# Two bits per step in the sample's threshold search, and a new set of stream priorities

## The chip, the core and the metric

The kernel runs on one core of a Trainium2 chip. Time is the device time of one execution in microseconds (us); a run's time is compared with the median of several runs. An engine's clock, where it is named, is the share of its full rate that the profile shows as granted to TensorE (PE).

## The reference

A decoder of two layers takes one step for two groups of rows: a prompt of 512 rows, and a sample of 8 requests with 4 new rows each (32 rows) that have 2048 earlier keys in a paged cache. In each layer a mixer A (gated MLP) and a mixer B (sparse attention) run side by side. Mixer B is where the change lies: a light indexer scores all keys of a row, the best are kept, and attention runs over these alone.

```
def indexer_scores(qi, wi, ki):
    s = jnp.einsum('bthd,bld->bthl', qi, ki).astype(jnp.float32) * (IDX_DIM ** -0.5)
    w = wi.astype(jnp.float32) * (IDX_HEADS ** -0.5)
    return jnp.einsum('bthl,bth->btl', jax.nn.relu(s), w)
...
    I = indexer_scores(qi, wi, ki_all)        # sample: 2052 keys per row
    ...
    _, idx = lax.top_k(I, TOPK_SAMPLE)        # the 256 best (prompt: the 128 best of up to 512)
    ...
    return attend_selected(q, k_sel, v_sel, valid)
```

After the mixers come the output projection w_o, a layer norm (LN1), a squared-ReLU MLP (f1, f2) with a gate, and a second layer norm.

## The kernel before

The 544 rows are held as columns in two halves of 272. Matrices are split into a high and a low part, and three products (`mm<-hi,Ah`, `hi,Al`, `lo,Ah` and the like) make one exact product on PE; VectorE (DVE) makes the low parts (L738), ScalarE (ACT) the high ones (L732). Each layer has, in order of time: the input projection; a stretch in which the indexer scores come out and are searched; a stretch of attention "units" (softmax heads, L1607 to L1621) with the sample's own attention (`s_attn`, `s_attn_f`) and the first half of w_o (L1918); the second half of w_o (L1928), which needs the sample's attention; LN1; the MLP (some 395 us); LN2.

The prompt's top-k takes 16 rounds of MAX8 (L1248) and MATCH_REPLACE8 (L1250) on DVE for each of three blocks of 512, 384 and 256 keys, and ends in masks (L1253). The softmax of a unit (L1607 first, then L1611 on ACT, L1613 and L1617) needs such a mask, but for the first block, which has no search.

The sample's choice works in another way, in `s_scores`. All scores of a row stand in `y.I` (L1306), 513 columns on each partition with a row's keys spread over several partitions. Their 256th largest value is found bit by bit: one ACT pass gives the signs of (threshold minus score) with a sum along the row (L1321); one PE matmul with a matrix `gallf` of ones and zeros adds the sums of the partitions of a row and gives each of them the total; two DVE instructions (L1334, L1336) compare the total with a limit and set the threshold's next bit. One round for the sign and 31 for the bits are 32 rounds per layer, one behind the other. Then 0/1 masks, ties and the mask `y.maskb` follow (L1339 to L1393, 22 DVE instructions and six matmuls). PE spreads this mask over the heads in matmuls `at<-maskb,sel` and the sample's attention goes on (L1855, L1880, up to `Al` at L1830).

The order of all instructions on all engines is fixed when the kernel is built. A planner (`Sched`) holds one generator per piece of work (a stream); each yields the engine and the cost in ns of its next piece, and the planner takes, in its own reckoning of time, the streams by a priority from the table `PR` (L59). So one changed number in `PR` may move instructions of all streams on all engines. Inside `count` the cost of a Sign pass is 707 ns with a margin `MARGIN` of 500 ns behind it before the matmul may be put in PE's list.

Of the kernel before, what the change touches and what calls it, by code (L numbers as in the profile page):

```python
# [55 lines left out]
GL = 1200.0  # L56
WP = 0.928
WO = 10.5
PR = {'q_sample': 13.5, 'free_raw': 8.0, 'gmix': 7.5, 'evac_c1': 14.0, 's_scores': 17.0, 's_block': 17.5, 'mix_b': 4.5, 'load_r': 6.5, 'kidx': 7.5, 's_attn': 5.0, 'evac_au': -2.5, 'head': 1.5, 's_kt': 6.0, 'loads': 7.5, 'evac_q': -4.0, 'sgu_load': 13.5, 's_relu': 1.0, 'mix_a': 14.5, 'setup1': 8.5, 's_attn_f': 10.5, 'gmlp': 4.5, 'unit': 9.0, 'load_pe': 13.0, 'evac_oa': -0.5, 'backbone': -5.5, 'evac_c0': -3.5, 'setup2': -2.0, 'splits': -2.5, 's_qk': 3.5, 'gnorm': 3.0, 'store': 3.0, 'setup': 13.0, 'wout22': 11.5, 'wadd': 12.0, 'mtee': 4.0, 'fin': 0.5, 'wsum': 7.0, 'wcopy': 0.5, 'evac_p': 10.0, 'ln1': 2.0, 'moving': 11.5, 'vload': 2.5, 'split_x': -1.0, 'evac_f2': 0.0, 'warm': 7.5, 'wsplit': 6.0, 'mv': 5.0, 'evac_o': 9.5, 'wout': 11.5, 'ln2': 10.5, 'evac_g': 0.0}  # L59
TBS = (3, 1, 2, 0)  # L60
BIAS = 65.107
GBIAS = 422.464
# [29 lines left out]
class Sched:  # L92
# [166 lines left out]
def cQ(cols, k=1):  # L259
    return [("Q", 480.0 * k), ("D", cols * 512 / 360.0)]  # L260
# [153 lines left out]
def build(tc, I, O, cols):  # L414
    nc = tc.nc
    V, A, G, PE, SP = nc.vector, nc.scalar, nc.gpsimd, nc.tensor, nc.sync
# [13 lines left out]
    def const(name, shape, dt=F32):  # L430
        return sb.tile(list(shape), dt, tag=name, name=name)
# [18 lines left out]
    gallf = const("gallf", [128, 128])  # L450
# [89 lines left out]
    def setup2():  # L540
        st = yield Al("w", [128, 2 * NT])
        yield cQ(768)
        SP.dma_start(st[:, :768], I["cbf"][:, :768])
        S.cur.ready += 900.0
        yield [("G", 3000.0)]
        G.tensor_copy(gall, st[:, 0:128])
        G.tensor_copy(gallf, st[:, 0:128])
# [282 lines left out]
    def mm(out, l, r, start, stop):  # L830
        PE.matmul(out, l, r, start=start, stop=stop, skip_group_check=True)  # L831
# [322 lines left out]
    def evac_c0(y, bi, ps):  # L1154
# [9 lines left out]
        if bi == 0:  # L1164
# [101 lines left out]
    def s_scores(y):  # L1266
# [40 lines left out]
        S.free(pi)  # L1307
        Iv = y.I[:, :513]
        cnt = sm("cnt", [128, 1], F16)
        cf = sm("cf", [128, 1])  # L1310
        c = sm("c", [128, 1], I32)
        d = sm("d", [128, 1], I32)
        c2 = sm("c2", [128, 1])
        c3 = sm("c3", [128, 1])
        ps = yield Al("at", [128, 512])
        dp = ps[:, 8:9].bitcast(I32)
        lim = NQ - 2 * STOP + 0.5

# [33 lines left out]
        thr = c3  # L1352
# [812 lines left out]
    def backbone():  # L2165
        for y in LY:
# [300 lines left out]
```

## Time and profile before

| What | us |
|---|---|
| median of 3 runs (lowest, highest) | 1471.88 (1468.57, 1473.65) |
| profiled execution | 1471.24 |
| its span, first to last instruction | 1469.5 |
| PE busy | 1427.5 (97%) |
| DVE busy | 1083.2 (74%) |
| ACT busy | 805.4 (55%) |
| granted PE clock, mean | 0.991 |

The shares of busy time are means over stages that differ. The search of the sample's threshold runs at 80 to 178 us in layer 0 and at 807 to 912 us in layer 1; the unit stages follow up to 271 and 996 us. A stage is read in the rows of the view by stretches: busy time of every engine in it, with the number of instructions in brackets, and the clock granted to PE.

### The profile page before, as it was taken

The page shows a single profiled execution, that of the slowest core. Times are in us where ns is not written, and L with a number is a line of the kernel's source. Part 1 is how long each engine was busy: PE and PEld are TensorE (multiplying, and loading weights), DVE is VectorE, ACT ScalarE, POOL GpSimd, SP SyncE. Part 2 cuts the span into 40 slices and gives each one's busy share as a digit, 9 for nine tenths or more (in the row PEclk, how much of TensorE's full clock was granted, in tenths as well). Part 3 has the DMA queues.
Part 4 walks back from the last instruction along what each step waited for, and adds up shares of the span by engine and source line. Part 5 has one row for each costly group of instructions (what it writes and reads, how often), then busy time and mean ns, then how long its engine had stood idle before and what let it go on. Part 6 is the DMA issues. An engine that isn't in the chain of part 4 may idle for free.

```text
span 1469.5 us, 31243 instructions
## 1 busy us (share of the span) xinstructions
PE 1427.5 (97%) x12284; PEld 1363.9 (93%) x12284; DVE 1083.2 (74%) x2812; ACT 805.4 (55%) x1895; POOL 143.8 (10%) x201
## 2 busy tenths in 40 slices
PE   9999989999999999999999988999999999999997
PEld 8798877999999999999987987889999999999996
DVE  5699995797956748567676999768979476494765
ACT  6668664473733626335466777755647255271533
POOL 2113512010000000000102045020000000000000
PEclk9999989999999999999999999999999999999999
DMA  7636424122231322313344265150223323132211
GB/s 241 220 102 203 168 87 160 47 71 87 92 124 58 130 72 87 128 60 118 113 133 163 96 214 178 58 189 30 79 88 108 101 72 130 59 115 87 87 58 62
DMA packets 55475, 164.48 MB, mean 112 GB/s; under 512 B 7648, under 2 KB 15008, under 8 KB 55328
## 3 DMA queue, kind: packets, MB, share of 16 engines
q1 hardware_dynamic: 44960, 124.73, 25.4%
q0 software_dynamic: 10368, 37.75, 7.9%
q8 instruction: 96, 1.57, 0.5%
q14 instruction: 51, 0.42, 0.1%
HBM read 156.09 MB, written 6.37 MB: 111 GB/s over the span
## 4 chain that ended last, share of the span: by engine, by line
PE 79%; DVE 15%; ACT 3%; issue 1%; DMA 1%; another core or an unknown queue 0%; SPq 0%; DVEq 0%; ACTq 0%
PE at L831 40%; PE mm L831 36%; DVE u L1250 3%; DVE m L1248 3%; DVE lo L738 1%; PE at L1621 1%; DVE u L1607 1%; DVE t L968 1%; PE at L1880 1%; DVE c L1336 1%; DVE u L1577 0%; DVE t L966 0%; PE at L1713 0%; DMA Bh<-in_x 0%; DVE w L868 0%
## 5 line engine op out<-in xcount | busy, mean ns | idle before, releaser
L732 ACT CAST hi<-raw 128x1024 fp32r<-128x1024 f32 (+5 forms) x137 | 139.0, 1019 | 178.3 <-PE mm L831 90.6
L738 DVE TENSOR_TENSOR lo<-raw,hi 128x1024 fp32r<-128x1024 f32 (+5 forms) x136 | 161.9, 1190 | 36.3 <-ACT hi L732 35.7
L831 PE MATMUL mm<-Bh,hi 128*128 128x272 f32 x584 | 172.0, 294 | 2.4 <-DVE t L1029 1.3
L831 PE MATMUL mm<-Ah,hi 128*128 128x272 f32 x584 | 170.7, 292 | 0.1
L831 PE MATMUL mm<-Bl,hi 128*128 128x272 f32 x584 | 169.0, 289 | 0.0
L831 PE MATMUL mm<-Bh,lo 128*128 128x272 f32 x584 | 168.6, 289 | 0.0
L831 PE MATMUL mm<-Al,hi 128*128 128x272 f32 x584 | 168.6, 289 | 0.0
L831 PE MATMUL mm<-Ah,lo 128*128 128x272 f32 x584 | 168.1, 288 | 0.0
L831 PE MATMUL at<-w,hi 128*128 128x272 f32 x704 | 158.9, 289 | 0.0
L691 ACT CAST hi<-u 128x512 fp32r<-128x512 f32 x128 | 75.4, 619 | 97.2 <-PE mm L831 40.9
L831 PE MATMUL at<-w,lo 128*128 128x272 f32 x416 | 119.8, 288 | 0.0
L831 PEld LDWEIGHTS at<-w,hi 128*128 128x128 f32 x704 | 119.4, 188 | 0.0
L2092 DVE TENSOR_TENSOR u<-u,mm 128x272 f32<-128x272 f32 x96 | 41.8, 436 | 103.2 <-PE mm L831 102.9
L831 PEld LDWEIGHTS mm<-Bh,hi 128*128 128x128 f32 x584 | 110.5, 189 | 4.1 <-ACT wi L1160 1.7
L831 PEld LDWEIGHTS mm<-Ah,hi 128*128 128x128 f32 x584 | 109.9, 188 | 1.3 <-issue 0.8
L831 PEld LDWEIGHTS mm<-Bh,lo 128*128 128x128 f32 x584 | 110.6, 189 | 0.1
L691 ACT CAST hi<-raw 128x1024 fp32r<-128x1024 f32 x64 | 53.2, 831 | 104.2 <-PE at L831 35.5
L831 PEld LDWEIGHTS mm<-Ah,lo 128*128 128x128 f32 x584 | 110.1, 189 | 0.2
L831 PEld LDWEIGHTS mm<-Bl,hi 128*128 128x128 f32 x584 | 110.2, 189 | 0.0
L831 PEld LDWEIGHTS mm<-Al,hi 128*128 128x128 f32 x584 | 109.8, 188 | 0.0
L831 PE MATMUL at<-Bl,hi 128*128 128x272 f32 x376 | 108.7, 289 | 0.0
L831 PE MATMUL at<-Al,hi 128*128 128x272 f32 x376 | 108.7, 289 | 0.0
(394 smaller groups left out, 4313.7 us busy)
## 6 DMA issues: line engine op xcount, KB each, us to landing
raw<-in_w_f SPq DMA_DIRECT2D x128, 512.0 KB
raw<-in_w_q SPq DMA_DIRECT2D x16, 512.0 KB
raw<-in_w_o SPq DMA_DIRECT2D x16, 512.0 KB
raw<-in_w_g SPq DMA_DIRECT2D x16, 512.0 KB
raw<-in_w_au SPq DMA_DIRECT2D x8, 512.0 KB
raw<-in_w_av SPq DMA_DIRECT2D x8, 512.0 KB
u<-in_x SPq DMA_DIRECT2D x8, 272.0 KB
hD<-t SPq DMA_DIRECT2D x16, 136.0 KB
```

Source lines behind the costliest of these rows:

```text
L691: A.copy(hi[:, :n], x)
L732: A.copy(c.hi[:, a:b], c.raw[:, a:b])
L738: E.tensor_tensor(c.lo[:, a:b], c.raw[:, a:b], c.hi[:, a:b].bitcast(F32), op=ALU.subtract)
L831: PE.matmul(out, l, r, start=start, stop=stop, skip_group_check=True)
L968: V.tensor_tensor(t[:, :n], t[:, :n], pb[:, :n], op=ALU.mult)
L1248: V.max(m8, work[:, :N])
L1250: V.match_replace(work[:, :N], m8, work[:, :N], -3.3e38)
L1336: V.scalar_tensor_tensor(c, dp, (2 ** (bit - 1)) if bit else 0, c, op0=ALU.bitwise_xor, op1=ALU.bitwise_xor)
L1607: V.tensor_tensor_reduce(P[:, :N], p[:, :N], bias[:, :N], scale=-0.125, scalar=3e38, op0=ALU.add, op1=ALU.min, accum_out=mx)
L1621: PE.transpose(p[:, c * 128:(c + 1) * 128], P[:, c * 128:(c + 1) * 128], ident)
L1880: PE.transpose(p[:, t, :], y.S[:, f, h2, q * 4 + t].rearrange("p a b -> p (a b)"), ident)
L2092: V.tensor_tensor(r[:, a:b], r[:, a:b], ps[:, :n], op=ALU.add)
```

## The change

Each step of the search sets two bits. A step makes three counts, for the three thresholds that the two bits allow: three Sign passes write three columns of `cf`, which is half precision now, as the sums of 513 signs are whole numbers that fit; one matmul with the half-precision matrix `gall` adds them (`gallf` goes). One DVE instruction counts how many of the three totals are over the limit, two turn that number into bits, and a fourth (`pre`) prepares the next step's three thresholds out of a table `tab` in PSUM, which 19 DVE instructions fill at the start of each layer's search. One round for the sign, 15 for two bits each and one for the last bit make 17 rounds per layer in place of 32, with 47 Sign passes in place of 32. The table `PR` gets new numbers for 31 of its 51 streams, so all five engines get a new order. In the changed kernel L1321 is L1329, and L1336, L1607, L1617, L1450, L1918, L1339 and L1393 are L1349, L1625, L1635, L1468, L1936, L1357 and L1411.

```
-PR = {'q_sample': 13.5, ..., 's_scores': 17.0, ..., 's_attn': 5.0, 'evac_au': -2.5, ..., 'unit': 9.0, ...}
+PR = {'q_sample': 13.5, ..., 's_scores': 18.0, ..., 's_attn': 3.0, 'evac_au': 9.5, ..., 'unit': 8.0, ...}
...
-        cf = sm("cf", [128, 1])
-        c = sm("c", [128, 1], I32)
+        cf = sm("cf", [128, 3], F16)
+        c = sm("c", [128, 3], I32)
...
+        tab = ps[:, 16:64].bitcast(I32).rearrange("p (k j) -> p k j", j=3)
+        yield [("V", 70.0 * 19)]
+        for j in range(3):
+            V.memset(tab[:, 0, j:j + 1], (j + 1) * 2 ** 29)
+        for i in range(1, 15):
+            V.tensor_scalar(tab[:, i, :], tab[:, i - 1, :], 0.25, None, op0=ALU.mult)
+        V.memset(tab[:, 15, :], 1)
+        V.tensor_copy(pre, tab[:, 0, :])
...
-        def count(thr):
-            yield [("A", 707.0)]
-            A.activation(y.maskb, Iv, AF.Sign, scale=-1.0, bias=thr, accum_out=cf)
+        def count(*thr):
+            for j, t in enumerate(thr):
+                yield [("A", 707.0)]
+                with nc.allow_low_precision(reason="sums of 513 signs are exact"):
+                    A.activation(y.maskb, Iv, AF.Sign, scale=-1.0, bias=t, accum_out=cf[:, j:j + 1])
             S.cur.ready += MARGIN
             yield [("P", 140.0)]
-            mm(ps[:, 0:1], gallf, cf, True, True)
+            mm(ps[:, :len(thr)], gall, cf[:, :len(thr)], True, True)
...
-        for bit in range(30, -1, -1):
-            yield from count(c.bitcast(F32))
+        for i in range(15):
+            k = 29 - 2 * i
             yield [("V", 70.0)]
-            V.tensor_scalar(dp, ps[:, 0:1], lim, float(2 ** bit), op0=ALU.is_gt, op1=ALU.mult)
+            V.scalar_tensor_tensor(pre, tab[:, i + 1, :], 2 << k, c[:, 0:1].to_broadcast([128, 3]), op0=ALU.bitwise_xor, op1=ALU.bitwise_xor)
+            yield from count(*(c[:, j:j + 1].bitcast(F32) for j in range(3)))
             yield [("V", 70.0)]
-            V.scalar_tensor_tensor(c, dp, (2 ** (bit - 1)) if bit else 0, c, op0=ALU.bitwise_xor, op1=ALU.bitwise_xor)
+            V.tensor_scalar(ps[:, 4:7], ps[:, 0:3], lim, None, op0=ALU.is_gt, op1=ALU.add, accum_out=c2)
+            yield [("V", 70.0)]
+            V.tensor_scalar(di, c2, float(2 ** k), None, op0=ALU.mult)
+            yield [("V", 70.0)]
+            V.tensor_tensor(c, di.to_broadcast([128, 3]), pre, op=ALU.bitwise_xor)
```

DVE's list in layer 0, where the first unit's softmax maximum stands (ISA rows of L1607 before). Before, the search and the mask are over at this place, and what stands in front of it is the queries' evacuation (L1450):

```order
L1450 TENSOR_TENSOR u_2362<-t_2235,u_2362 128x2x128
L1450 TENSOR_TENSOR u_2380<-t_2283,u_2380 128x2x128
L1450 TENSOR_TENSOR u_2456<-t_2331,u_2456 128x2x128
L1450 TENSOR_TENSOR u_2503<-t_2375,u_2503 128x2x128
L1607 ISA u_2914,mx_2939<-at_2918,cp 128x128
L1607 ISA mx_2939 128x1
```

Now the list holds rounds of the search (L1345, L1347, L1349, L1342) behind the first units, which have come as far as their scaling (L1631, L1635):

```order
L1468 TENSOR_TENSOR u_2342<-t_2175,u_2342 128x2x128
L1635 TENSOR_SCALAR u_2754<-u_2754,su_2779 128x128
L1631 RECIPROCAL su_2781<-su_2781 128x1
L1936 SCALAR_TENSOR_TENSOR u_2480<-u_2480,mm_2765 128x272
L1345 TENSOR_SCALAR at_1495,c_1493<-at_1495 128x3
L1347 TENSOR_SCALAR at_1495<-c_1493 128x1
L1349 TENSOR_TENSOR c<-at_1495,pre 128x3
L1342 SCALAR_TENSOR_TENSOR pre<-at_1495,c 128x3
L1631 RECIPROCAL su_2790<-su_2790 128x1
```

Over the whole list the last mask instruction (L1393, now L1411) stood 16 rows ahead of the first maximum and stands 84 rows behind it.

DVE's list in layer 1, at the first unit's maximum, before; the search's last two rounds (L1334, L1336) stand on both sides of it:

```order
L1334 TENSOR_SCALAR at_10528<-at_10528 128x1
L1336 SCALAR_TENSOR_TENSOR c<-at_10528,c 128x1
L868 COPY u_11582<-at_11998 128x512
L1450 TENSOR_TENSOR u_11592<-t_11463,u_11592 128x2x128
L1450 TENSOR_TENSOR u_11739<-t_11610,u_11739 128x2x128
L1607 ISA u_12029,mx_2939<-at_12033,cp 128x128
```

The same place now (L1468 was L1450, L1936 was L1918, L866 was L868):

```order
L1936 SCALAR_TENSOR_TENSOR u_11837<-u_11837,mm_11983 128x272
L1468 TENSOR_TENSOR u_11578<-t_11315,u_11578 128x2x128
L866 COPY Ah_9979<-at_11931 128x8x64
L1468 TENSOR_TENSOR u_11584<-t_11510,u_11584 128x2x128
L1468 TENSOR_TENSOR u_11708<-t_11557,u_11708 128x2x128
L1468 TENSOR_TENSOR u_11722<-t_11609,u_11722 128x2x128
L1468 TENSOR_TENSOR u_11936<-t_11651,u_11936 128x2x128
L1345 TENSOR_SCALAR at_10784,c_1493<-at_10784 128x3
L1347 TENSOR_SCALAR at_10784<-c_1493 128x1
L1349 TENSOR_TENSOR c<-at_10784,pre 128x3
L866 COPY u_11584<-at_12081 128x512
L1936 SCALAR_TENSOR_TENSOR u_11840<-u_11840,mm_12066 128x272
```

Here the search still ends about where the first unit begins, but more evacuations and copies have moved ahead of both: the last mask instruction stood 45 rows behind the first maximum, and stands 44 behind it.

PE's list at one count of layer 0, before: one fp32 matmul, in two passes of its own, between products:

```order
L831 MATMUL mm_2071<-lo_1838,Ah_146 128x256
L831 MATMUL at_1196<-cf,gallf 128x1
L831 MATMUL mm_2071<-hi_1809,Ah_146 128x256
L831 MATMUL mm_2071<-hi_1809,Al_147 128x256
L831 MATMUL mm_2071<-lo_1838,Ah_146 128x256
```

And now: one half-precision matmul of three columns, with a weight load of its own:

```order
L829 MATMUL mm_2370<-lo_2024,Ah_145 128x256
L829 LDWEIGHTS gall
L829 MATMUL at_1495<-cf,gall 128x3
L829 MATMUL mm_2370<-hi_1980,Ah_145 128x256
L829 MATMUL mm_2370<-hi_1980,Al_146 128x256
L829 MATMUL mm_2370<-lo_2024,Ah_145 128x256
```

## Rows read from the trace of the kernel before

**Rows 1.** The page, busy time of each engine over the span:
```profile
PE 1427.5 (97%) x12284; PEld 1363.9 (93%) x12284; DVE 1083.2 (74%) x2812; ACT 805.4 (55%) x1895; POOL 143.8 (10%) x201
```

**Rows 2.** Stretches: us, busy us of PE, PEld, DVE, ACT, POOL; PEclk; DMA; GB/s:
```profile
85.00:195.00 110.00, 106.85 (x1078) 100.07 (x1076) 106.52 (x366) 78.63 (x230) 38.77 (x51) 1.00 0.50 164
195.00:270.00 75.00, 67.51 (x755) 56.09 (x756) 51.88 (x206) 46.26 (x134) 7.49 (x8) 0.91 0.31 106
325.00:720.00 395.00, 395.00 (x3150) 394.79 (x3149) 267.44 (x511) 179.49 (x364) 0.00 (x0) 1.00 0.28 90
735.00:804.00 69.00, 65.85 (x522) 55.64 (x522) 47.77 (x144) 47.49 (x114) 7.59 (x15) 1.00 0.46 149
804.00:912.00 108.00, 101.84 (x1035) 94.66 (x1034) 104.33 (x349) 80.00 (x233) 41.53 (x54) 1.00 0.47 156
912.00:994.00 82.00, 75.86 (x862) 65.16 (x861) 59.01 (x223) 51.50 (x146) 10.60 (x12) 0.96 0.39 131
```

**Rows 3.** Waits of DVE, 804 to 912 us: total us, times, longest:
```profile
DVE u L1236 <- ACT u L1230: 0.7, 1, 0.7
```

**Rows 4.** Search lines L1321 and L1334: ns min/median/max, first and last start:
```profile
L1321 ACT ACTIVATE maskb<-u,c x62: 710/728/743, 84.4 to 909.1; 128x513 bf16<-128x513 f32 x62
L1321 ACT ACTIVATION_READ_ACCUMULATOR maskb<-u,c x62: 185/187/207, 85.0 to 909.7; 128x1 f32 x62
...
L1334 DVE TENSOR_SCALAR at<-at x62: 142/156/168, 86.8 to 911.2; 128x1 int32<-128x1 f32 x62
```

**Rows 5.** Timeline of PE around two counts: start us, us, instruction:
```profile
101.11 0.28 PE L831 MATMUL at<-cf,gallf 128*128 128x1 f32 x2
101.25 0.37 PE L831 MATMUL mm<-hi,Ah 128*128 128x256 f32 x1
101.46 0.28 PE L831 MATMUL mm<-hi,Al 128*128 128x256 f32 x1
101.58 0.28 PE L831 MATMUL mm<-lo,Ah 128*128 128x256 f32 x1
...
178.67 0.16 PE L831 MATMUL at<-cnt,gall 128*128 128x1 f16 x1
...
178.90 0.29 PE L831 MATMUL mm<-Ah,lo 128*128 128x272 f32 x1
```

**Rows 6.** Groups of DVE by form: busy us, mean ns, idle before:
```profile
L738 DVE TENSOR_TENSOR lo<-raw,hi 128x1024 fp32r<-128x1024 f32 x123 | 150.7, 1225 | 34.4 <-ACT hi L732 34.0
...
L868 DVE COPY w<-at 128x512 f32<-128x512 f32 x20 | 13.3, 679 | 0.0
...
L1450 DVE TENSOR_TENSOR u<-t,u 128x256 fp32r<-128x256 f32 x16 | 6.5, 438 | 0.0
```

**Rows 7.** The mask's last instruction (L1393), ns, first and last start:
```profile
L1393 DVE TENSOR_SCALAR maskb<-u x2: 144/145/146, 189.2 to 926.4; 128x1 bf16<-128x1 f32 x2
```

**Rows 8.** Line L1607, first start; timeline, layer 1's first unit, mask matmuls, first L1928:
```profile
L1607 DVE CUSTOM_DVE_ANT_0 u<-at,cp x16: 272/284/292, 195.5 to 988.4; 128x128 f32<-128x128 f32 x16
...
910.43 0.28 DVE L1607 CUSTOM_DVE_ANT_0 u<-at,cp 128x128 f32<-128x128 f32 x1
...
198.91 0.27 PE L831 MATMUL at<-maskb,sel 128*128 128x1 bf16 x4
...
927.12 0.25 PE L831 MATMUL at<-maskb,sel 128*128 128x1 bf16 x4
...
271.33 0.44 DVE L1928 SCALAR_TENSOR_TENSOR u<-u,mm 128x272 f32<-128x272 f32 x1 [1.10 <-PE mm L831]
...
995.65 0.44 DVE L1928 SCALAR_TENSOR_TENSOR u<-u,mm 128x272 f32<-128x272 f32 x1 [0.57 <-PE mm L831]
```

**Rows 9.** Stretches of 5 us in layer 0's unit stage:
```profile
210.00:215.00 5.00, 2.10 (x14) 1.69 (x15) 4.94 (x20) 4.88 (x11) 0.00 (x0) 0.89 0.00 0
215.00:220.00 5.00, 5.00 (x33) 4.04 (x34) 4.72 (x18) 3.58 (x12) 0.00 (x0) 0.77 0.02 5
```

**Rows 10.** Waits of PE, 800 to 920 us: total us, times, longest:
```profile
PE at L831 <- ACT maskb L1321: 1.3, 1, 1.3
```

More of the change, by code (lines that the diff above doesn't have):

```diff
@@ L58 @@
 WO = 10.5
-PR = {'q_sample': 13.5, 'free_raw': 8.0, 'gmix': 7.5, 'evac_c1': 14.0, 's_scores': 17.0, 's_block': 17.5, 'mix_b': 4.5, 'load_r': 6.5, 'kidx': 7.5, 's_attn': 5.0, 'evac_au': -2.5, 'head': 1.5, 's_kt': 6.0, 'loads': 7.5, 'evac_q': -4.0, 'sgu_load': 13.5, 's_relu': 1.0, 'mix_a': 14.5, 'setup1': 8.5, 's_attn_f': 10.5, 'gmlp': 4.5, 'unit': 9.0, 'load_pe': 13.0, 'evac_oa': -0.5, 'backbone': -5.5, 'evac_c0': -3.5, 'setup2': -2.0, 'splits': -2.5, 's_qk': 3.5, 'gnorm': 3.0, 'store': 3.0, 'setup': 13.0, 'wout22': 11.5, 'wadd': 12.0, 'mtee': 4.0, 'fin': 0.5, 'wsum': 7.0, 'wcopy': 0.5, 'evac_p': 10.0, 'ln1': 2.0, 'moving': 11.5, 'vload': 2.5, 'split_x': -1.0, 'evac_f2': 0.0, 'warm': 7.5, 'wsplit': 6.0, 'mv': 5.0, 'evac_o': 9.5, 'wout': 11.5, 'ln2': 10.5, 'evac_g': 0.0}
+PR = {'q_sample': 13.5, 'free_raw': 8.0, 'gmix': 7.5, 'evac_c1': 14.5, 's_scores': 18.0, 's_block': 17.5, 'mix_b': 2.5, 'load_r': 9.0, 'kidx': 8.0, 's_attn': 3.0, 'evac_au': 9.5, 'head': 1.5, 's_kt': 6.0, 'loads': 8.5, 'evac_q': -4.0, 'sgu_load': 9.0, 's_relu': 2.0, 'mix_a': 14.5, 'setup1': 4.5, 's_attn_f': 11.0, 'gmlp': 7.5, 'unit': 8.0, 'load_pe': -1.5, 'evac_oa': 0.0, 'backbone': -5.5, 'evac_c0': -3.5, 'setup2': -3.0, 'splits': -2.5, 's_qk': 2.0, 'gnorm': 6.0, 'store': 3.0, 'setup': 9.0, 'wout22': 11.5, 'wadd': 12.0, 'mtee': 4.0, 'fin': -2.0, 'wsum': 0.0, 'wcopy': 2.0, 'evac_p': 10.0, 'ln1': 2.5, 'moving': 9.5, 'vload': 3.5, 'split_x': -1.0, 'evac_f2': 9.0, 'warm': 13.0, 'wsplit': 6.5, 'mv': 5.0, 'evac_o': 9.5, 'wout': 12.0, 'ln2': 6.5, 'evac_g': 0.0}
 TBS = (3, 1, 2, 0)
@@ L449, in build @@
     gall = const("gall", [128, 128], F16)
-    gallf = const("gallf", [128, 128])
     gneg = const("gneg", [128, 128], F16)
@@ L546, in setup2 @@
         G.tensor_copy(gall, st[:, 0:128])
-        G.tensor_copy(gallf, st[:, 0:128])
         G.tensor_copy(gneg, st[:, 128:256])
@@ L1309, in s_scores @@
         cnt = sm("cnt", [128, 1], F16)
-        cf = sm("cf", [128, 1])
-        c = sm("c", [128, 1], I32)
-        d = sm("d", [128, 1], I32)
+        cf = sm("cf", [128, 3], F16)
+        c = sm("c", [128, 3], I32)
         c2 = sm("c2", [128, 1])
@@ L1315, in s_scores @@
         ps = yield Al("at", [128, 512])
-        dp = ps[:, 8:9].bitcast(I32)
-        lim = NQ - 2 * STOP + 0.5
-        def count(thr):
-            yield [("A", 707.0)]
-            A.activation(y.maskb, Iv, AF.Sign, scale=-1.0, bias=thr, accum_out=cf)
+        di = ps[:, 8:9].bitcast(I32)
+        pre = sm("pre", [128, 3], I32)
+        tab = ps[:, 16:64].bitcast(I32).rearrange("p (k j) -> p k j", j=3)
[6 more added lines that the diff above has]
+        V.tensor_copy(pre, tab[:, 0, :])
+        lim = NQ - 2 * STOP + 0.5
+        def count(*thr):
[3 more added lines that the diff above has]
+                    A.activation(y.maskb, Iv, AF.Sign, scale=-1.0, bias=t, accum_out=cf[:, j:j + 1])
             S.cur.ready += MARGIN
             yield [("P", 140.0)]
-            mm(ps[:, 0:1], gallf, cf, True, True)
+            mm(ps[:, :len(thr)], gall, cf[:, :len(thr)], True, True)
             S.cur.ready += 100.0
@@ L1328, in s_scores @@
         yield [("V", 270.0)]
-        V.tensor_scalar(d, ps[:, 0:1], lim, -float(2 ** 31), op0=ALU.is_gt, op1=ALU.mult)
-        V.tensor_scalar(c, d, 31, 2 ** 30, op0=ALU.arith_shift_right, op1=ALU.bitwise_xor)
-        for bit in range(30, -1, -1):
-            yield from count(c.bitcast(F32))
+        V.tensor_scalar(di, ps[:, 0:1], lim, -float(2 ** 31), op0=ALU.is_gt, op1=ALU.mult)
+        V.scalar_tensor_tensor(c, di.to_broadcast([128, 3]), 31, pre, op0=ALU.arith_shift_right, op1=ALU.bitwise_xor)
+        for i in range(15):
+            k = 29 - 2 * i
             yield [("V", 70.0)]
-            V.tensor_scalar(dp, ps[:, 0:1], lim, float(2 ** bit), op0=ALU.is_gt, op1=ALU.mult)
+            V.scalar_tensor_tensor(pre, tab[:, i + 1, :], 2 << k, c[:, 0:1].to_broadcast([128, 3]), op0=ALU.bitwise_xor, op1=ALU.bitwise_xor)
+            yield from count(*(c[:, j:j + 1].bitcast(F32) for j in range(3)))
             yield [("V", 70.0)]
-            V.scalar_tensor_tensor(c, dp, (2 ** (bit - 1)) if bit else 0, c, op0=ALU.bitwise_xor, op1=ALU.bitwise_xor)
+            V.tensor_scalar(ps[:, 4:7], ps[:, 0:3], lim, None, op0=ALU.is_gt, op1=ALU.add, accum_out=c2)
[3 more added lines that the diff above has]
+            V.tensor_tensor(c, di.to_broadcast([128, 3]), pre, op=ALU.bitwise_xor)
+        c = c[:, 0:1]
+        yield from count(c.bitcast(F32))
+        yield [("V", 140.0)]
+        V.tensor_scalar(di, ps[:, 0:1], lim, None, op0=ALU.is_gt)
+        V.tensor_tensor(c, di, c, op=ALU.bitwise_xor)
         thr = c.bitcast(F32)
```

## The prediction

> **What bounds the kernel now.** I read the page first: PE is busy for 97% of the span [rows 1], so no change can take more than some 40 us of waits, unless it takes work from PE. Then the view by stretches [rows 2], which shows where these waits are. In the MLP, 325 to 720 us, PE is busy for 395.00 of 395 us. What is open lies in the search and unit stages: PE is idle for 3.2 and 7.5 us in layer 0 (85 to 195 and 195 to 270 us), for 3.2, 6.2 and 6.1 us in layer 1 (735 to 804, 804 to 912, 912 to 994 us), and the clock loses 9% of 75 us and 4% of 82 us, 6.8 and 3.3 us.
>
> The rows to look at are those of the search. At 85 to 195 us DVE is busy for 106.5 of 110 us, at 804 to 912 us for 104.3 of 108, and its waits in the latter are not worth a name, 0.7 us the longest [rows 3]. So there DVE is full: when a softmax or the sample's mask is ready is set by how much stands ahead of it in DVE's list. The 366 instructions of 85 to 195 us, each at the mean of its group, sum to 127.5 us and take 110, since neighbours overlap: 0.863 us of time for 1 us of durations. In layer 1 it is 0.889 (117.4 in 104.3).
>
> The search itself is a chain, Sign, count, two DVE instructions, 32 times. It ran from 80 to 178 and from 807 to 912 us, and ACT waited for its threshold. With DVE full beside it, it doesn't set the end of the stage alone.
>
> **The change part by part.**
>
> *Counts on PE.* A count in fp32 starts at 101.11 us; the second product behind it starts at 101.46, and the usual gap of two such products is 0.12 (101.46 to 101.58) [rows 5]. So it takes 0.35 - 0.12 = 0.23 us. The same reckoning from two products ahead to four behind, over all 64 counts, has a median of 0.22, so 64 take 14 us. A half-precision count, at 178.67, lets the second product start at 178.90: 0.23 - 0.13 = 0.10 us (0.13 is 395.00 us by 3150 matmuls, most of these products of 272 columns [rows 2]). It stood in no dense row, so it may be as dear as the fp32 one. 34 counts take 3.4 to 7.5 us. PE saves 6.6 to 10.7 us over both layers. As the lower bound I take no saving, which a count of 14 / 34 = 0.4 us would mean, if the weight load, an instruction of its own now, breaks the row of products. I take 6.6, 3.3 per layer, since the counts in question stand between products as the fp32 ones do.
>
> *Sign passes on ACT.* 30 more, at 728 + 187 ns with the read of the sum [rows 4]: 27.5 us, 13.7 per layer. ACT has 78.6 and 80.0 us of 110 and 108 [rows 2], so it rises to 84 and 87% and still isn't full. I cost it at nothing; the cover is ACT's idle time, 31 and 28 us, and where that isn't beside the right round the price is that of a rival below.
>
> *Round work on DVE.* 62 pairs of 156 ns instructions go; 60 fours of the same size come (128x1 and 128x3 cost the start of an instruction and little else), then 2 x 19 for the table. At 0.15 each, per layer: 9.3 us go, 9.0 come for rounds and 2.6 for the table: +2.3 us. Bounds: 0 (table at 0.07 each, as two neighbours are issued) and +4 (the accumulating compare gets a read of its own of some 0.08).
>
> *What the priorities move, layer 0.* I took the order of DVE's list and gave each instruction the mean of its group [rows 6]. Ahead of the first softmax maximum there were 191.3 us, now 183.2: out go six evacuations of queries (0.438 each), three low parts (1.225), five w_o rows, the whole mask chain and two rounds; in come seven copies of 128x512 (0.679 each) and smaller ones. So the first units may begin 8.1 x 0.863 = 7 us earlier than 195.5 [rows 8]. The sample's mask is the other side: 184.0 us of DVE work stood ahead of its last instruction, now 209.8. That is 25.7 x 0.863 = 22 us later if DVE is as full as before. The mask was done at 189.2 us [rows 7] and PE took it at 198.9 [rows 8], a slack of 9.7. So PE's mask matmuls come 12 us later at most. At least they come 3 us later: they stand 2 us later in PE's own list. I take 9, as some of the work moves to where DVE is not full, before 85 us.
>
> From there to the first row of the second half of w_o (L1928, 271.3 us [rows 8]) PE had 72.4 us. It has 3.3 (counts) + 2 (moved ahead) = 5.3 us less to do. And of the 7.5 us idle a fuller PE list gives back between 0 and all; I take 3. Layer 0: 9 - 5.3 - 3 = +0.7 us; ends 3 - 5.3 - 7.5 (I stop at -5, since the softmaxes still come one after the other) and 12 - 5.3 = +7.
>
> *Layer 1.* Ahead of the first maximum stand 172.6 us of DVE work of this layer, before 158.0: five copies of 128x512 (3.4), two low parts (2.45), two copies to `Ah` (1.4), three evacuations (1.3), the search (2.3), the rest small. 14.7 x 0.889 = 13 us later, less about 2 that fit in DVE's idle time at 735 to 804 us, where it is busy for 47.8 of 69 [rows 2]: +11 us on 910.4 [rows 8]. The mask has 13.6 us more ahead of it and no slack, done at 926.4 and used at 927.1: +10, and I take +9. Again PE has 5.3 us less to do behind it, and it gives back 0 to 6.1 us of idle time and some of the 3.3 of the clock; I take 2, since DVE is still busy for 59 of 82 us there. Layer 1: 9 - 5.3 - 2 = +1.7 us; ends -4 and +6.
>
> *The rest.* 48 relu pieces of the MLP go from ACT to DVE (24 a layer, 0.44 each); DVE is busy there for 267 of 395 us [rows 2] and PE waits for nothing: 0.
>
> *Sum.* +0.7 + 1.7 = +2.4 on the profiled 1471.24, 1473.6; the median of the runs is 0.6 above the profiled one, so 1474.
>
> **The rivals.**
>
> *PE's saving comes through whole.* If PE's own list sets the end of both unit stages, the later mask costs nothing, and PE gains 6.6 us of counts and 4 of the 13.6 us of idle time in the two unit stages: 1471.9 - 10.6 = 1461. For it: PE is 90 and 93% busy in these stages [rows 2], and in layer 0 there is unit work 7 us earlier. Against it: the second half of w_o needs the sample's attention, and that starts with the mask.
>
> *The mask's delay stands.* A chain in layer 0 as in layer 1: mask, spread, scores, exponentials, transposes, products, w_o's second half. If the units in front run out of work, PE idles where it was busy, and nothing is given back: +12 - 5.3 and +11 - 5.3, and with that a lower clock: 1471.9 + 12.4 = 1484, and a few more for the clock. It decides when the mask comes more than 8 us after PE is ready for it. What the clock does then shows in layer 0: in 210 to 215 us PE was busy for 2.10 of 5 us, and in 215 to 220 us its clock was 0.77 [rows 9], 1.2 us lost. By the Trainium skill's page "TensorE: Matmul & The Clock Gate", section "HAM oscillation — how this bites in real kernels", pauses of PE are paid a second time, by products at half rate behind them; the trace agrees, with those 0.77 behind the pause. By that rule a pause of 9 us per layer would make this rival some 2 to 7 us dearer than its waits (6.8 us is what the clock lost in the whole unit stage of layer 0), and it speaks against a change that moves the pause to one place.
>
> *Three Signs in a row hold PE up.* The count's place in PE's list was set with 0.707 us a pass; the rows say 0.915. Three passes are 0.62 us later than reckoned, and all of PE's list stands behind the count. If each of 30 counts waits for that, 19 us: 1490. Before, the same error of 0.21 a pass led to 1.3 us of waits in one place [rows 10], as the margin of 0.5 us covers it; it does not cover 0.62 in full. I price it at 30 x 0.3 = 9 us: 1481.
>
> *It changes nothing.* The search was hidden by DVE's other work, and the priorities trade one stretch for the other: that is within my own case.
>
> **How the numbers follow.** A measurement of this kernel tells 0.3%, 4.4 us, from no change. My forecast, 1474 (1467.5 to 1476.3), has 0.36; PE's saving in full, 1461, 0.31; the mask's delay, 1484, 0.21; the Signs, 1481, 0.11; 0.01 is left. So faster 0.32, the same 0.36, slower 0.32. Cases of both signs hold most of the chance, so the range is wide: 1459 to 1487. It leaves out a tenth at each end. The ends of my own case add up to -9 and +13 over both layers; as both are hardly at one end together, its own range is 1466 to 1481.
>
> **What would show it.** First unit at about 188 us in layer 0 (195.5 before) and 921 in layer 1; mask matmuls at 208 and 936; first L1928 at 272 and 998; DVE full from some 80 us to the first unit in both layers; PE's idle time ahead of the mask matmuls up, and behind them down; the counts' waits for ACT under 3 us. I am wrong if the first unit of layer 1 is not later, if the mask matmuls move by less than 3 us, if the second half of w_o starts where only counts moved it (-3 us in each layer), or if ACT's Sign shows up among the largest waits of PE.

## The result and the profile after

The changed kernel takes 1488.45 us (median of 6 runs, 1483.19 to 1490.50), the kernel before 1473.13 (6 runs, 1468.57 to 1475.64): 1.0102 of the time before, 95% interval 1.0090 to 1.0115. It is slower by 1.0%, 15 us. I had forecast no change at 1474, and 1459 to 1487 as the range.

The page of the changed kernel, first the busy time over the span:

```profile
span 1486.7 us, 31079 instructions
...
PE 1430.8 (96%) x12189; PEld 1360.9 (92%) x12190; DVE 1104.8 (74%) x2921; ACT 808.5 (54%) x1891; POOL 141.9 (10%) x199
```

DVE has 21.6 us more than in [rows 1]; the granted clock fell from 0.991 to 0.982 in the mean. The stretches that answer to [rows 2] (same columns), cut at 60 us and then at events: scores of layer 0 done, first unit, second half of w_o, second layer norm, and the same three for layer 1:

```profile
0.00:60.00 60.00, 52.43 (x388) 46.88 (x389) 33.49 (x117) 35.49 (x77) 12.05 (x32) 0.95 0.64 215
60.00:109.80 49.80, 48.37 (x380) 40.08 (x378) 45.21 (x111) 29.76 (x87) 10.09 (x12) 1.00 0.38 127
109.80:194.50 84.70, 78.30 (x797) 71.52 (x798) 80.51 (x291) 70.13 (x192) 36.17 (x48) 0.94 0.54 179
194.50:283.50 89.00, 78.32 (x850) 66.32 (x849) 62.98 (x246) 54.75 (x151) 11.12 (x12) 0.94 0.34 115
283.50:734.40 450.90, 450.81 (x3612) 450.34 (x3611) 321.85 (x665) 205.55 (x413) 10.29 (x11) 1.00 0.28 91
734.40:842.30 107.90, 102.14 (x795) 89.02 (x798) 80.14 (x233) 68.62 (x183) 13.01 (x23) 0.97 0.41 134
842.30:935.60 93.30, 83.11 (x843) 73.26 (x835) 89.07 (x334) 78.50 (x217) 32.52 (x44) 0.95 0.50 163
935.60:1014.30 78.70, 73.93 (x838) 63.17 (x837) 58.21 (x226) 51.83 (x146) 11.03 (x13) 0.98 0.38 123
```

The MLP is as long as before and full. All the loss lies in the two mixer stretches, each from a layer's start to its second half of w_o. Before, that half began at 271.3 us [rows 8] in layer 0, and in layer 1 273.1 us behind the start of the layer norm that stands ahead of it; now it is 283.5 and 279.9. That is +12.2 and +6.8 us; the rest of the span gives 1.8 back.

The same two stretches in one row each, first of the kernel before, then of the changed one:

```profile
0.00:271.30 271.30, 256.50 (x2458) 226.11 (x2459) 213.37 (x724) 181.51 (x486) 67.90 (x102) 0.97 0.49 164
722.60:995.70 273.10, 255.83 (x2512) 226.53 (x2511) 223.21 (x751) 190.20 (x521) 63.40 (x84) 0.99 0.46 152
```

```profile
0.00:283.50 283.50, 257.42 (x2411) 224.80 (x2412) 222.19 (x762) 190.13 (x505) 69.43 (x102) 0.95 0.47 157
734.40:1014.30 279.90, 259.19 (x2467) 225.46 (x2467) 227.43 (x791) 198.95 (x545) 56.56 (x79) 0.96 0.43 141
```

These four rows hold the balance of PE. It is idle for 26.1 + 20.7 us where it was 14.8 + 17.3: +14.7. Its clock takes another 13.5 us or so: 0.982 over the span of 1486.7 us is 26.8 us below full rate, 0.991 over 1469.5 was 13.2. (The rows above give it to two digits only.) The stretches are 19.0 us longer, so what is left, PE's work at full clock, is some 9 us less, within the 6.6 to 10.7 that I had allowed for the counts.

Where in the stretches it lies shows when they are cut at the first mask matmul, first in the kernel before, then in the changed one:

```profile
0.00:198.91 198.91, 191.55 (x1729) 172.38 (x1729) 164.45 (x539) 139.13 (x364) 60.41 (x94) 0.99 0.56 189
198.91:271.33 72.42, 64.98 (x736) 53.76 (x731) 48.93 (x189) 42.38 (x123) 7.49 (x8) 0.92 0.29 97
722.60:927.12 204.52, 190.83 (x1730) 169.33 (x1728) 174.49 (x569) 146.84 (x403) 55.84 (x76) 0.98 0.49 161
927.12:995.70 68.58, 65.00 (x791) 57.20 (x784) 48.72 (x183) 43.36 (x119) 7.56 (x8) 1.00 0.37 126
```

```profile
0.00:217.98 217.98, 199.75 (x1729) 175.53 (x1730) 181.03 (x609) 153.89 (x407) 61.91 (x94) 0.96 0.51 170
217.98:283.48 65.50, 57.65 (x682) 49.25 (x682) 41.14 (x154) 36.24 (x98) 7.52 (x8) 0.92 0.34 115
734.40:948.51 214.11, 196.30 (x1719) 171.07 (x1719) 181.20 (x615) 155.80 (x425) 49.05 (x71) 0.96 0.45 146
948.51:1014.31 65.80, 62.89 (x748) 54.40 (x748) 46.23 (x178) 43.15 (x120) 7.51 (x8) 0.97 0.38 123
```

Ahead of the mask matmuls the stretches are 19.1 and 9.6 us longer, with 10.9 and 4.1 us more of idle PE and a lower clock. Behind them they are 6.9 and 2.8 us shorter. So PE loses the time before it comes to the mask.

The idle time is many small waits. In the view of PE's waits of these stretches there were 38 before, 31 us in all; now there are 66, 46 us, and none longer than 2.7. The largest of the changed kernel, over the span (total us, times, longest):

```profile
PE at L829 <- DVE u L1029: 4.7, 2, 2.7
PE at L1639 <- DVE u L1635: 3.0, 4, 1.3
PE at L829 <- issue: 2.7, 4, 1.0
PE at L1110 <- DVE t L1107: 2.3, 2, 2.1
...
PE at L829 <- DVE pre L1322: 1.6, 1, 1.6
...
PE at L829 <- DVE maskb L1411: 1.1, 1, 1.1
...
PE at L829 <- ACT maskb L1329: 0.7, 2, 0.4
```

Some are of the table's making. In layer 1 these are the wait for `pre` and part of that for L1029, the rotation of the queries, which stood shortly behind the table there. DVE there, start and duration:

```profile
842.31 0.69 DVE L1304 TENSOR_SCALAR u<-at 128x512 f32<-128x512 f32 x1 [0.30 <-PE at L829]
...
843.44 2.82 DVE L1320 TENSOR_SCALAR at<-at 128x3 int32<-128x3 int32 x14
...
846.44 0.16 DVE L1322 COPY pre<-at 128x3 int32<-128x3 int32 x1
846.51 0.68 DVE L1023 TENSOR_TENSOR u<-at,cp 128x512 f32<-128x512 f32 x1
...
847.97 0.69 DVE L1029 TENSOR_TENSOR u<-u,u 128x512 f32<-128x512 f32 x1
```

Fourteen scalings, each of the row before it, take 0.2 us each, 2.82 in a row. In layer 0 L1029 ran ahead of the table, and it was a low part (L736) behind the table that PE waited 1.5 us for. Without the table (e4 below) the waits for `pre` and for that low part are gone, and the one for L1029 in layer 1 is 0.7 us in place of 2.0.

The waits come back as clock, but not at a fixed rate. Layer 0's pause at the head of the search, where PE waited 2.7 us for L1029 and 1.5 for the low part, and the clock that PE was granted there, a mean of its two levels, 1.2 and 2.4 GHz (row as in rows 2):

```profile
100.00:120.00 20.00, 15.62 (x91) 9.25 (x88) 19.16 (x70) 11.52 (x32) 7.26 (x7) 0.79 0.79 292
```

By the page "TensorE: Matmul & The Clock Gate" of the Trainium skill, section "HAM oscillation — how this bites in real kernels", pauses are paid twice. Here the trace agrees for this pause, with 4.4 us of idle time and the 0.79. Over both stretches it agrees only in part: in the changed kernel 14.7 us more of idle time go with some 13.5 of clock, but in e9 below 16.6 more go with some 5.

In layer 0 the search is not shorter. It ran from 80.7 to 177.8 us, and now from 110.5 to 207.3: 97.1 and 96.8 us. There 32 rounds of 3.0 us became 17 of 5.7, of which three Signs with their reads take 2.8 where one took 0.8. In layer 1 it is 11 us shorter: from 807.5 to 911.6 us before, 104.1 us, and now from 843.0 to 936.4, 93.4. The first Sign and the last instruction of the search, before:

```profile
L1321 ACT ACTIVATE maskb<-u,zero x2: 728/728/728, 80.7 to 807.5; 128x513 bf16<-128x513 f32 x2
...
L1336 DVE SCALAR_TENSOR_TENSOR c<-at,c x62: 135/158/161, 87.0 to 911.4; 128x1 int32<-128x1 int32 x62
```

The same two now (L1329 for zero, L1354), with the instructions of a step between them, and the mask's last; ns min/median/max, first and last start:

```profile
L1329 ACT ACTIVATE maskb<-u,zero x2: 727/727/727, 110.5 to 843.0; 128x513 bf16<-128x513 f32 x2
...
L1329 ACT ACTIVATE maskb<-u,c x92: 709/728/755, 117.9 to 934.2; 128x513 bf16<-128x513 f32 x92
...
L1345 DVE TENSOR_SCALAR_CACHE_REDUCE at<-at x30: 146/157/170, 124.7 to 933.4; 128x3 f32<-128x3 f32 x30
L1345 DVE DVE_READ_ACCUMULATOR at<-at x30: 128/140/146, 124.8 to 933.5; 128x1 f32 x30
...
L1347 DVE TENSOR_SCALAR at<-c x30: 140/161/164, 125.0 to 933.6; 128x1 int32<-128x1 f32 x30
...
L1349 DVE TENSOR_TENSOR c<-at,pre x30: 138/160/163, 125.2 to 933.9; 128x3 int32<-128x3 int32 x30
...
L1354 DVE TENSOR_TENSOR c<-at,c x2: 157/157/157, 207.1 to 936.3; 128x1 int32<-128x1 int32 x2
...
L1411 DVE TENSOR_SCALAR maskb<-u x2: 136/150/163, 217.8 to 948.3; 128x1 bf16<-128x1 f32 x2
```

The last row answers to [rows 7]: the mask is done 28.6 us later in layer 0, and 21.9 later in layer 1, of which 11.8 are layer 0's.

### The profile page after: what moved, and what is told of

Read it like the earlier page. It is cut to its first block, busy times and chain, and to the rows that moved or that the text cites. A ratio compares the mean times of both kernels' runs of the same rounds, so it can differ in the third digit from the quotient of the medians.

```text
span 1486.7 us, 31079 instructions
## 1 busy us (share of the span) xinstructions
PE 1430.8 (96%) x12189; PEld 1360.9 (92%) x12190; DVE 1104.8 (74%) x2921; ACT 808.5 (54%) x1891; POOL 141.9 (10%) x199
## 4 chain that ended last, share of the span: by engine, by line
PE 79%; DVE 13%; ACT 4%; issue 2%; DMA 1%; SPq 0%; ACTq 0%; DVEq 0%
PE at L829 39%; PE mm L829 37%; DVE u L1248 2%; DVE m L1246 2%; DVE lo L736 1%; PE at L1731 1%; PE at L1639 1%; DVE u L1625 1%; PE at L1898 1%; DVE w L866 1%; ACT maskb L1329 1%; DMA Bh<-in_x 1%; DMA raw<-in_w_c 1%; DVE u L1595 0%; ACT u L868 0%
## 5 line engine op out<-in xcount | busy, mean ns | idle before, releaser
L736 DVE TENSOR_TENSOR lo<-raw,hi 128x1024 fp32r<-128x1024 f32 (+4 forms) x136 | 162.4, 1195 | 36.9 <-ACT hi L730 35.3
```

The source lines that it names most:

```text
L736: E.tensor_tensor(c.lo[:, a:b], c.raw[:, a:b], c.hi[:, a:b].bitcast(F32), op=ALU.subtract)
```

## The experiments

All ratios are to the kernel before, run beside it on the same chip, with 95% intervals. The chips differ: the kernel before took 1464.5 us on the chip of e12 to e15, and 1472.2 to 1473.3 on the others, so runs are compared by their ratios. In all runs but those named otherwise the lists of all engines are the same as in the kernel that was edited, but for the edited instructions.

**Search or priorities.** Each alone: the new search with the old `PR`, and the old search with the new one. (Both lists are new then, since the planner starts from other costs.)

```
-PR = {new}   +PR = {old}      # in the changed kernel: e1
-PR = {old}   +PR = {new}      # in the kernel before:  e2
```

Expected of e1: 

> The new search with the old priorities. The median of the kernel before is 1473, of the changed kernel 1488. Theory A (the new priorities place the search and the sample's mask late, and with them the second half of w_o): without them the loss is gone, 1470 to 1477, less the counts' saving and plus some 3 us per layer of DVE time for the table. Theory B (the new search itself costs the time: 3.4 us of table per layer on a full DVE in a chain of 0.2 us each, rounds of 0.7 us in place of 0.33): 1482 to 1490.

Expected of e2: 

> The old search (32 rounds, fp32 counts) with the new priorities. Theory A (priorities): most of the loss is there, 1482 to 1490. Theory B (search): near the kernel before, 1469 to 1476.

Measured: e1 1493.6 us, 1.0140 (1.0122 to 1.0158); e2 1539.2 us, 1.0443 (1.0426 to 1.0461). Neither theory holds. The new search with the old priorities is dearer than with the new ones, so with this search the new priorities are the better by 5 us; with the old search they cost 66. The two do not add up.

**Half-precision counts.**

```
-        cf = sm("cf", [128, 1])
+        cf = sm("cf", [128, 1], F16)
-            mm(ps[:, 0:1], gallf, cf, True, True)
+            mm(ps[:, 0:1], gall, cf, True, True)
```

> The kernel before with half-precision counts alone, 64 of them; all else in the same order. If PE's time in the search stretch counts and a half-precision count is the cheaper by 0.12 us: 64 x 0.12 = 7.7 us less, 1465. If DVE's full list sets the end of the stretch, or the counts cost the same: 1471 to 1474, no change.

Measured: 1472.4 us, 0.9997 (0.9988 to 1.0007). In the trace a count costs 0.125 us by the reckoning of the prediction, where the fp32 one costs 0.227 (medians over 64). 6.5 us less work on PE, no time gained: PE's work on the counts doesn't set the time in the old order.

**The table.** Filled once at the kernel's start, in SBUF:

```
     V.memset(zero, 0.0)
+    tab = const("tab", [128, 16, 3], I32)
+    ...                                     # the 18 instructions, once
...
-        tab = ps[:, 16:64].bitcast(I32)...  # and the 18 instructions per layer
```

> The changed kernel with the table filled once, at the kernel's start, in SBUF, and only the copy to pre left in each layer; the order of everything else is the same. Theory B: 18 DVE instructions, 3.3 us per layer, leave a stretch where DVE is full and PE waits for what stands behind them (1.6 us for the table itself, 2.7 and 2.0 us for the query's rotation behind it): 1488 less 5 to 9, 1479 to 1483. Theory A: the mask's place decides, 1485 to 1488.

Measured: 1481.2 us, 1.0060 (1.0039 to 1.0080): 0.4% below the changed kernel, as the theory that the table costs time by itself had it.

**No rounds: what each order costs without its search.** The Signs, counts and DVE instructions of the rounds are left out, their places stay booked.

```
-                    A.activation(y.maskb, Iv, AF.Sign, ...)
+                    if t is zero: A.activation(y.maskb, Iv, AF.Sign, ...)
...                  # the same for the matmul; the DVE lines of the loop go
```

Changed kernel, with the table: 

> The changed kernel without the rounds of the search (no Signs but the first, no counts behind it, no round work on DVE; the table stays), so that its threshold is not the reference's; all other instructions in the same order. Chain theory (the end of the search, which begins 30 us later than before and lasts as long, sets when the mask comes, and the mask sets the second half of w_o): the mask comes some 20 us earlier, both unit stages end 6 to 12 us earlier, 1465 to 1475. Order theory (the new order of the rest costs the time, whatever the search does): 1480 to 1488.

Kernel before: 

> The same with the kernel before: no rounds, the rest in its order. If both kernels pay about the same for their search, as the equal length of 97 us says, this gains as much as the changed kernel without rounds does, and the difference of the two floors, up to 15 us, is what the order alone costs. If the old search was hidden by DVE's other work: 1468 to 1474.

Changed kernel, without the table too: 

> The changed kernel without rounds and without the table (a threshold that is not the reference's), in its order. The table took 7.3 us and the rounds 11.5; if they add up: 1469 to 1471, and the order alone is 12 us longer than the old one without rounds (1457.9). If they overlap: 1472 to 1476.

Measured: e5 1476.9 us, 1.0027 (1.0016 to 1.0037); e6 1457.9 us, 0.9890 (0.9874 to 0.9907); e15 1464.0 us where the kernel before took 1464.5, 0.9991 (0.9977 to 1.0005). (e5 lies between the ranges of its two theories.) These three carry the main finding. The search costs 1.0102 / 0.9991 = 1.1% in the changed kernel, table included, and 1 / 0.9890 = 1.1% in the kernel before: each search costs as much in the order that was planned for it. And the new order, with no search in either, is 0.9991 / 0.9890 = 1.0% longer than the old, as much as the whole loss. The two floors ran on different chips; on one chip, e5 is 19 us above e6, with the table in it, which e4 puts at some 6.

This is one way to split the loss, and the other way does not agree with it. Where the new search stands in the old order (e10 below), it costs 1.0117 / 0.9890 = 2.3%, twice what it costs in its own, and all of the loss is there without the new order. So the two parts are not terms of a sum: the new order alone is 1.0% longer, and the old order with the new search in it loses as much.

**The chain of the search.** One Sign per step in place of three:

```
-                    A.activation(y.maskb, Iv, AF.Sign, scale=-1.0, bias=t, accum_out=cf[:, j:j + 1])
+                    if j == len(thr) - 1: A.activation(...)
```

> The changed kernel with one Sign pass per round in place of three (two of the three columns of counts stay zero, so the threshold is wrong); the order is the same. Chain theory: a round is 1.9 us shorter, 15 rounds 28 us per layer, and the mask comes earlier until DVE's list holds it: 1470 to 1479. Fullness theory (DVE's list alone sets the mask, as I predicted): DVE has the same work, 1484 to 1489.

Measured: 1488.2 us, 1.0094 (1.0078 to 1.0111), no gain. ACT has 43 us less in the two mixer stretches (190.1 + 199.0 before the edit):

```profile
0.00:284.60 284.60, 259.29 (x2411) 226.46 (x2412) 223.49 (x762) 167.77 (x445) 70.27 (x102) 0.95 0.46 156
735.60:1015.90 280.30, 259.93 (x2466) 226.91 (x2466) 226.97 (x792) 177.81 (x485) 59.29 (x79) 0.96 0.42 140
```

DVE's and PE's times are nearly what they were. The chain theory falls: the search ran from 111.2 to 208.4 us in layer 0, as long as with three Signs, and a count started 1.8 us behind the end of its Sign, where it had been 0.8 (medians). So in this order the three Signs don't set the length of a step; its places in DVE's and PE's lists do.

**DVE's share of a round.** Two of the four instructions left out:

```
-            V.scalar_tensor_tensor(pre, tab[:, i + 1, :], 2 << k, ...)
-            V.tensor_scalar(di, c2, float(2 ** k), None, op0=ALU.mult)
-            V.tensor_tensor(c, di.to_broadcast([128, 3]), pre, op=ALU.bitwise_xor)
+            V.tensor_tensor(c, c2.bitcast(I32).to_broadcast([128, 3]), pre, op=ALU.bitwise_and)
```

> The changed kernel with two of the four DVE instructions of a round (the scaling and the next step's thresholds are left out, so the threshold is wrong); the order is the same. It takes 0.27 us per round from a full DVE, 4 us per layer, and 0.2 us of it from the chain. Chain theory and fullness theory both say 3 to 7 us less, 1481 to 1485; if it is no less than 1487, small DVE instructions between others cost nothing, and the table's 7 us came from its place at the head of the search.

Measured: 1485.7 us, 1.0073 (1.0041 to 1.0105), with runs from 1476.9 to 1491.3. It may be 3 us or nothing.

**The new search in the old order.** Each step takes the places of two old rounds:

```
+            yield from count((0, 1), 3)     # two Signs in the first round's place
...          # pre
+            yield from count((2,), 3)       # the third Sign and the count in the second's
...          # compare, scale, xor
```

Table once: 

> The new search in the old order: each two-bit step takes the places of two old rounds in the lists (two Signs and pre in the first, the third Sign, the count and the rest in the second), every other instruction stands as before; the table is filled once at the kernel's start. If the order of the rest costs what the changed kernel lost (floors without rounds 1457.9 and 1476.9): 1468 to 1475, near the kernel before, with 30 counts a kernel less on PE and some 2 us per layer more on DVE. If the new search is dear by itself: 1478 or more.

Table per layer: 

> The same, with the table filled in PSUM at the head of each layer's search as in the changed kernel. The table took 7 us there; if a full DVE pays for it in any order: 4 to 8 us above the run with the table filled once. If it was dear only for what stood behind it in the new order: 0 to 2 us above.

Table once, one Sign per step: 

> The new search in the old order with the table filled once, and one Sign pass per step in place of three (two columns of counts stay zero, the threshold is wrong). With three it took 1486.8. If the two added passes, in a row on ACT ahead of what PE and DVE wait for, are what the old order cannot take: 1470 to 1477. If it is the round's DVE work (0.72 us where two old rounds had 0.6): 1483 to 1488.

Measured: e9 1486.8 us, 1.0097 (1.0083 to 1.0111); e10 1489.4 us, 1.0117 (1.0100 to 1.0134); e12 1469.3 where the kernel before took 1464.5, 1.0021 (1.0007 to 1.0035). The old order doesn't hold the new search either, against my expectation. Here it is the Signs: without two of three, three quarters of the loss are gone (e12 ran on another chip than e9). In that order PE waits for ACT for 7.7 us in the search of layer 0 (80 to 200 us), where it had waited for 2.0; the longest:

```profile
PE at L1737 <- ACT Bh L874: 2.6, 1, 2.6
PE at L835 <- ACT maskb L1326: 2.4, 4, 1.1
PE mm L835 <- ACT t L1460: 1.8, 1, 1.8
```

The two mixer stretches of e9:

```profile
0.00:280.20 280.20, 255.59 (x2411) 222.11 (x2412) 220.06 (x758) 192.51 (x516) 65.95 (x101) 0.97 0.46 159
731.50:1010.10 278.60, 254.55 (x2465) 222.84 (x2464) 225.64 (x766) 200.65 (x551) 61.76 (x84) 0.98 0.44 149
```

PE is idle for 48.7 us in them, 1.9 more than in the changed kernel, but its clock over the span is 0.988, where that kernel has 0.982.

**The front's priorities.** In the changed kernel, ten of the streams back to the old numbers (lists change).

```
-PR = {..., 'setup': 9.0, 'setup1': 4.5, 'sgu_load': 9.0, 'load_pe': -1.5, ...}
+PR = {..., 'setup': 13.0, 'setup1': 8.5, 'sgu_load': 13.5, 'load_pe': 13.0, ...}
```

> The changed kernel with the old priorities for the streams that load and prepare at the front (setup, setup1, setup2, warm, sgu_load, load_pe, load_r, loads, kidx, vload); the rest of the table is new. In the first 60 us the new order leaves PE 3.4 us more idle and its clock at 0.95. If the front's streams are the cause: 1480 to 1484. If the order within the search and unit stages is: 1486 to 1492, or any time of another order.

Measured: 1491.9 us, 1.0134 (1.0113 to 1.0155). The front is mended, 55.77 us of PE in the first 60 at full clock, where the changed kernel has 52.43 at 0.95, and the time is lost elsewhere:

```profile
0.00:60.00 60.00, 55.77 (x432) 47.23 (x436) 34.13 (x119) 39.18 (x89) 11.48 (x33) 1.00 0.62 210
```

**The wait for the mask.** The mask matmuls read a constant:

```
-                       y.maskb[:, (2 * h2 + qd) * 128:(2 * h2 + qd + 1) * 128], True, True)
+                       sel.rearrange("p a b c -> p (a b c)")[:, (2 * h2 + qd) * 128:...], True, True)
```

Changed kernel: 

> The changed kernel with a constant in place of the sample's mask as the operand of the mask matmuls (attention runs over other keys, so the result differs); search and mask are still computed, nothing of the sample's attention waits for them, and the order is the same. If the mask's lateness sets the end of the unit stages: both end 5 to 9 us earlier, 1470 to 1478. If the softmaxes and evacuations in DVE's list set it as well: 1484 to 1489.

Kernel before: 

> The kernel before with the same constant. There the mask had 9.7 us to spare in layer 0 and none in layer 1, so 1466 to 1473: less than the changed kernel gains, if the mask's lateness is what the two differ in.

Measured: e13 1482.6 us where the kernel before took 1464.5, 1.0114 (1.0096 to 1.0131); e14 1465.0 us, 1.0005 (0.9995 to 1.0014). No gain in either. With no mask to wait for, the changed kernel's mask matmuls still began at 217.0 us in layer 0, 1 us earlier than with it (in layer 1 they came 4 us earlier, at a clock of 0.98 over that stretch where it was 0.96):

```profile
L829 PE MATMUL at<-sel x80: 163/219/314, 217.0 to 951.3; 128*128 128x128 bf16 x64, 128*128 128x1 bf16 x16
```

What stands ahead of them brings PE there late. Its wait for the late mask isn't the cause.

**Copies back to ACT.** The planner chooses ACT or DVE for each copy; in the two mixer stretches DVE had 62 and has 88. Every second large one goes to ACT, at its place:

```
         if (yield Alt([cC(n)], [cV(n)])):
-            V.tensor_copy(out, src)
+            ncp[0] += n == 512
+            if n == 512 and ncp[0] % 2: A.copy(out, src)
+            else: V.tensor_copy(out, src)
```

Changed kernel: 

> The changed kernel, its lists as they are, but every second copy of 128x512 that the planner gave to DVE is done by ACT at the same place (23 copies, 0.679 us each on DVE, 0.58 on ACT). With 30 more Sign passes booked on ACT the planner had given DVE 26 copies more ahead of the second half of w_o than before (62 to 88). If DVE's list up to there sets the time: 15.6 us of DVE work less, 8 to 14 us of time, a ratio to the kernel before of 1.001 to 1.005. If ACT, now with Signs and copies, holds PE up: 1.009 or more.

With the table once: 

> The same with the table filled once at the kernel's start. 5 to 7 us less than the run before it: 0.996 to 1.001 of the kernel before, and faster than it if both savings come in full.

Kernel before: 

> The kernel before with every second of its DVE copies of 128x512 on ACT (17 copies, 11.5 us of DVE work). If DVE's list sets the time there as well: 0.993 to 0.997 (4 to 10 us less). If the old order has ACT in the way where PE waits for these copies: 0.999 to 1.003.

Measured: e16 1490.2 us, 1.0119 (1.0098 to 1.0141); e17 1487.3 us, 1.0107 (1.0093 to 1.0121); e18 1473.1 us, 1.0011 (1.0001 to 1.0021). 11 us less of busy DVE in the changed kernel's mixer stretches and no gain; with the table out, it is slower than e4. DVE's total work is not borne out as the one cause; but ACT took over what DVE was rid of (400.1 us busy where it had 389.1), so a wait that only moved from DVE to ACT is not excluded. PE's clock was 0.94 and 0.97 in e16:

```profile
0.00:286.10 286.10, 259.37 (x2411) 227.09 (x2412) 215.05 (x748) 196.01 (x519) 70.55 (x102) 0.94 0.46 156
737.20:1016.60 279.40, 257.80 (x2467) 224.22 (x2466) 223.34 (x780) 204.04 (x557) 57.06 (x79) 0.97 0.42 141
```

No version with the new search beats the kernel before.

## Why the prediction was wrong

*Counts on PE.* Right in size: 0.125 and 0.227 us a count, and PE's work at full clock fell by some 9 us, within my 6.6 to 10.7. Wrong in place: I took 3.3 us per layer off PE's work behind the mask matmuls, and the counts all stand ahead of them (the last start at 206.3 and 935.6 us). Wrong in worth, as far as the old order goes: e3 saves 6.5 us of this work there and gains nothing.

*Signs on ACT at nothing.* Right in the new order, where e7 leaves 60 out and gains nothing; the rival of 0.3 us per count falls with it, 0.7 us of waits in two places. It is wrong for the old order (e12), which I had not asked about.

*Round work on DVE.* Mis-sized, though within my bounds. (The 60 fours of the prediction are 30 over both layers, and 19 instructions at 0.15 are 2.9, not 2.6.) I had +2.3 us of durations per layer. From start to next start the search takes 13.1 us of DVE per layer, where it took 9.35: +3.8. What I missed is that a chain of dependent small instructions doesn't overlap: 0.2 us for each of the table's, and 0.7 for a step. By the ratios the table is worth 5 to 6 us in this order (e4 against the changed kernel, e15 against e5), some 2 with the copies on ACT (e17 against e16), and some 3 in the old order (e9 against e10).

*Layer 0: first unit 7 us earlier, mask matmuls +9.* The first unit came at 194.5, 1 us earlier; the mask was done 28.6 us later where my upper end was 22, and its matmuls came at 218.0, 19.1 later. I had let some of the added work move to where DVE isn't full, before 85 us. It didn't: the scores were done, and DVE's part of the search began, at 109.8 in place of 80.0. But the late mask is not why the matmuls were late: PE waited 1.1 us for it.

*Layer 1: first unit +11, mask matmuls +9.* The first unit came at 935.6 and the mask matmuls at 948.5; less the 11.8 us that layer 0 had lost by then, +13.4 and +9.6. The reading of DVE's list was good for the first unit. That the mask matmuls agree with my +9 is in part luck: the view of PE's waits names none for the mask in layer 1, and 4.1 us more of other idle time, with the lower clock, brought PE there as late.

```profile
935.59 0.28 DVE L1625 CUSTOM_DVE_ANT_0 u<-at,cp 128x128 f32<-128x128 f32 x1
...
1014.31 0.44 DVE L1946 SCALAR_TENSOR_TENSOR u<-u,mm 128x272 f32<-128x272 f32 x1
```

*The step that failed* is the one that says when PE comes to the mask matmuls. I let the mask hold them up, by 9 us per layer, put PE's own list only 2 us later, and took every other wait to be as before. They came 19.1 and 9.6 us later, and the wait that I had priced is 1.1 us of it in layer 0; e13 shows that it was no term at all. What came in its place is other waits ahead of the mask matmuls, 9.8 and 4.1 us more, and the clock. The step behind it, that PE gives back idle time in both layers (3 and 2 us), failed as well: with less work there, the rest of the unit stages is 6.9 and 2.8 us shorter, where I had 8.3 and 7.3, and the idle time in it is 10.8 us where it was 11.0. In all, PE was idle for 14.7 us more and lost some 13.5 more to the clock. I had priced one wait and put at nothing what 31 new priorities do to all the others, which with the clock behind them is some +28 us.

None of my four signs of being wrong came up. All of them watch the first unit, the mask matmuls, the counts or the Signs, the parts that I had priced.

*The rivals.* The late mask at 1484 came nearest in time, and e13 refutes its mechanism. What I should have set up as the rival for the slower side is "more small waits all over and the clock behind them", with no single place.

What stays open is which of the new order's waits cause the others, and which of its priorities make them. The front, the mask, the Signs and the copies were each taken away alone, and none gave the time back; after the front and the copies, others took their place. The 21 changed priorities outside the front were not tried by themselves.

## What to carry to other kernels

Half the rounds is not half the search: in layer 0, 17 rounds of 5.7 us took as long as 32 of 3.0, and leaving two of three Signs out of a round did not shorten it, as long as the lists kept the round's places. Where a table of priorities sets the order of everything, run each order with the changed part left out, and the changed part in the old order too. The first gave all of the 1% to the order; the second lost as much in the old order. Either run alone would have named one cause, and the two together show that search and order do not add up. In a kernel whose PE is 97% busy, count the waits and the clock over a whole stretch and not the one wait that the change touches: a saving on PE of some 9 us was outweighed by 28 more waits, 14.7 us of idle time, and some 13.5 us of clock.

## What the runs showed of the hardware

A DVE instruction that does not need the small one before it starts some 0.07 us behind that one (846.44 to 846.51 us), one that does, 0.2: the table's fourteen took 2.82 us. An instruction that also gives out a sum is followed by a read of its own on DVE (140 ns, L1345). A half-precision count of one to three columns, with its own weight load, costs PE 0.125 us in a dense row of products, an fp32 one of one column 0.227. What PE's idle time costs in clock is no constant of the kernel: 16.6 us more of it went with some 5 us of lost clock in e9, and 14.7 with some 13.5 in the changed kernel.
